# Seven-product weight pairs in a decoder layer: four sums kept in PSUM, weight sums on VectorE

## Chip, core and metric

One core of a Trainium2 chip runs the whole layer as one program. The metric is the device time of one execution in microseconds. The core has five engines that run side by side, each through its own queue in order: TensorE (PE, matmuls into the PSUM banks), VectorE (DVE), ScalarE (ACT), GpSimd (POOL, which has no part in PSUM work here) and SyncE (SP), which here issues almost all DMAs.

## What is computed

A decoder layer for 1024 prompt positions and 8 samples, so 1032 columns, 1024 wide. One input projection (1024 x 6912) feeds three branches (window attention, a state-space layer, a gated MLP); each branch is read out, merged by sigmoid gates and projected, with a layer norm at the end. The part that matters here is the projection:

```
proj = jnp.einsum('ntd,de->nte', x, w_in)
q, k, v, z_a, u_b, z_b, u_c, v_c, z_c, g = jnp.split(proj, cuts, axis=-1)
...
vn = _layernorm(v_c);  y_c = u_c * (tril(W_s) vn + b);   silu(z_c) * y_c
gates = jax.nn.sigmoid(g)
```

## The kernel before

Every product is float32 made of three passes: an operand is split into a high part (an ACT copy to fp32r) and a low part (the difference), and `mm3` (L98) adds high x high, high x low and low x high in one PSUM bank. The high and low parts of a 128x512 weight come from `hilo` (L138): the ACT copy is L145, the subtraction L146 on whichever engine is given. Raw weights are loaded by SP into a pool of 5 buffers (`wraw`, L131), and split weights lie in 4 buffers each ("wh", "wl") or, every second one, in parts of the x tiles that are no longer needed ("strips", L952, L956; the trace names those `b`).

The order of execution is made by a scheduler that simulates the engines and takes instructions by priority, which is the order of the text except where `tc.high_priority()` lifts it. The result is one fixed list for each engine. A wait at the head of a list holds up all behind it.

In time the stages are: projections and the state-space layer (to about us 300); attention, with single projection chunks as filler (`fill`, L760; the attention's own DVE line that scales the scores is L731); then, from us 413 to 702, 13 "pairs"; then the readout and the output projection. Each pair computes two blocks of 128 output columns over all 1032 positions as a 2 x 2 block product (blocks of 512 inputs by 516 positions) in Winograd's form: seven products in place of eight. `half_sums` (L890) and L930 to L937 make the four sums of x beforehand (`Tx`). `pair` (L960) forms four sums of weights: s3 = a11 - a21, s1 = a21 + a22, s2 = s1 - a11, s4 = a12 - s2, all on POOL (trace line L263). A product (`prod`, L976) is two halves of 258 columns, one in a bank of the pool "mm" (3 banks), one in "ms" (4 banks), each with 12 matmuls. Every product takes new banks. The seven additions that make the four output blocks, each in two halves, are `add` (L1007, trace line L1010) on DVE: SBUF plus PSUM to SBUF tiles in `stg` (L948); only the first product P1 is copied out by ACT (L1019). The kinds of pairs are: two "v" (stored as they are), four "zu" (silu of `z` times `u`: ACT L999, DVE L1000 and L1004), seven "g" (tanh on ACT, L990, then stored, L991). `mid` and `ends` place the pieces of the gated MLP (L1055 to L1126) between the pairs.

Of the kernel before, what the change touches and what calls it, by code (L numbers as in the profile page):

```python
# [15 lines left out]
AF = mybir.ActivationFunctionType  # L16
OP = mybir.AluOpType
# [47 lines left out]
def decoder_step(ctx, tc, io):  # L65
    nc = tc.nc
    V, S, G, PE = nc.vector, nc.scalar, nc.gpsimd, nc.tensor
# [7 lines left out]
    pk = ctx.enter_context(tc.tile_pool(name="pk", bufs=4, space=bass.MemoryType.PSUM))  # L75
# [3 lines left out]
    def nm(s):  # L79
        cnt[0] += 1  # L80
        return f"{s}{cnt[0]}"

    def b2(dt=F32):
        return big.tile([128, B2], dt, tag="b2", name=nm("b"))

    def bank(pool=None, n=512):
        if pool is pk:
            t = pk.tile([128, 512], F32, tag="ms", name=nm("ms"), bufs=NMS)
        elif pool == "t":
            t = pk.tile([128, 512], F32, tag="mt", name=nm("mt"), bufs=NMT)  # L90
        else:
            t = pm.tile([128, 512], F32, tag="mm", name=nm("mm"), bufs=NMM)
        return t

    def ct(w=CW, rows=128):
        return tp.tile([rows, CW], F32, tag="ct", name=nm("ct"))

    def mm3(out, pairs, start=True, stop=True):  # L98
        n = len(pairs)
        for i, (ah, al, bh, bl) in enumerate(pairs):  # L100
            PE.matmul(out, ah, bh, start=start and i == 0, stop=False)  # L101
            PE.matmul(out, ah, bl, start=False, stop=False)  # L102
            PE.matmul(out, al, bh, start=False, stop=stop and i == n - 1)  # L103

    def f(ap):
        return ap.bitcast(F32)
# [101 lines left out]
    for k in range(8):  # L208
        for b in range(2):
            hi, lo = fgr[b][k // 4]  # L210
            ws = slice((k % 4) * 128, (k % 4) * 128 + 128)
            for c in range(NCH):
                ps = first[b * 3 + c][:, :CW]
# [48 lines left out]
    def TT(out, a, b, op, eng=None):  # L262
        (eng or V).tensor_tensor(out, a, b, op=op)  # L263
# [168 lines left out]
    for Er_, Ei_, base in ((Eb[:, 1], Eb[:, 0], 1), (Ea[:, 0], Ea[:, 1], 5)):  # L432
        V.memset(Er_[:, :, 0], 1.0)
        V.memset(Ei_[:, :, 0], 0.0)
        for lv in range(4):
            w = 1 << lv
# [5 lines left out]
    for n in (1, 2, 3, 4):  # L442
        o = cv[:, 0, :, n - 1]
# [3 lines left out]
        o = cv[:, 1, :, n - 1]  # L447
# [25 lines left out]
    us_ = [b2(), b2()]  # L473
# [173 lines left out]
    with tc.high_priority():  # L647
        for hf_ in range(2):
            tps = bank("t")
            for i in range(4):  # L650
                m = hf_ * 4 + i
# [91 lines left out]
    def values(m):  # L743

        q0, zo = NS + m * 128, (m % 2) * 1024
        z4 = v2(qzt[:, zo + 512:zo + 1024], 128)
        o = bank(pk)
        k_ = keys(m)[0] // 128
        for kb in range(k_, 2):
            for g in range(2):  # L750
                seq(PE.matmul(o[64 * g:64 * g + 64, :], vtok[:, m - 1 + kb, 64 * g:64 * g + 64],
                              scs[m % 2][:, g * 4:g * 4 + 4, kb * 128:(kb + 1) * 128], start=kb == k_, stop=kb == 1))
        done = V.scalar_tensor_tensor(z4, v2(o, 128), 0.5, z4, op0=OP.mult, op1=OP.mult)
        nc.sync.dma_start(yaD[:, :, q0:q0 + 128], z4)
        return done
# [52 lines left out]
    for i in range(4):  # L808
        for g in range(2):
            rs = slice(64 * g, 64 * g + 64)  # L810
            h = i + 4 * g
# [76 lines left out]
    HT, QT = T // 2, T // 4  # L888
# [9 lines left out]
    for m in range(NBLK):  # L898
# [16 lines left out]
        done = values(m)  # L915
# [15 lines left out]
    for n_, t_ in ((2, tf[2]), (3, tf[0]), (1, tf[1]), (4, tf[3])):  # L931
        h_, l_ = b2(F32R), b2(F32R)
        for k in range(4):
            o = slice(k * HT, (k + 1) * HT)
# [14 lines left out]
    stgs = [[stg[:, (2 * n_ + c) * QT:(2 * n_ + c + 1) * QT] for c in range(2)] for n_ in range(4)]  # L949
# [2 lines left out]
    strips = [tuple(x_[j][:, e * T + HT:e * T + HT + 512] for x_ in (xh, xl)) for j in range(2) for e in range(2)]  # L952
    wcnt = [0]
    mark = []

    def whl(raw, eng):  # L956
        wcnt[0] += 1
        return hilo(raw, eng, strips[wcnt[0] // 2 % 4] if wcnt[0] % 2 else None)

    def pair(kind, n1, n2, mid=()):  # L960
        i11, i12, i21, i22 = 2 * n1, 2 * n1 + 1, 2 * n2, 2 * n2 + 1
        a11, a21 = wraw(i11)[0], wraw(i21)[0]
        s3 = wraw()
        TT(s3, a11, a21, OP.subtract, G)
        a22 = wraw(i22)[0]
        TT(a21, a21, a22, OP.add, G)
        s1 = a21
        s2 = wraw()
        TT(s2, s1, a11, OP.subtract, G)
        w11 = whl(a11, G)  # L970
        a12 = wraw(i12)[0]
        s4 = wraw()
        TT(s4, a12, s2, OP.subtract, G)
        w2 = whl(s2, V)

        def prod(w, n_):  # L976
            ps = [bank()[:, :QT], bank(pk)[:, :QT]]
            for c in range(2):
                mm3(ps[c], [(w[0][:, k * 128:(k + 1) * 128], w[1][:, k * 128:(k + 1) * 128]) + bop(n_, k, c)
                            for k in range(4)])  # L980
            return ps

        p1, u2, c11, u3 = stgs

        done = {}

        def out(m, h, c, t_):
            hs_ = slice(h * HT + c * QT, h * HT + (c + 1) * QT)
            if kind == "g":
                S.activation(t_, t_, AF.Tanh, scale=0.5)  # L990
                nc.sync.dma_start(gD[(n1, n2)[m] - GG][:, hs_], t_)  # L991
                return
            if kind == "v":
                nc.sync.dma_start(vcD[:, (n1, n2)[m] - GVC, hs_], t_)
                return

            if m == 0:
                tg = ct()
                S.activation(tg[:, :QT], t_, AF.Tanh, scale=0.5)  # L999
                V.scalar_tensor_tensor(t_, tg[:, :QT], 1.0, t_, op0=OP.add, op1=OP.mult)  # L1000
            done[m, h, c] = t_
            if (1 - m, h, c) in done:
                z_, u_ = done[0, h, c], done[1, h, c]
                V.scalar_tensor_tensor(u_, z_, 0.5, u_, op0=OP.mult, op1=OP.mult)  # L1004
                nc.sync.dma_start(uszD[:, n1 - GZC, hs_], u_)

        def add(o, a, b):  # L1007
            for c in range(2):
                with tc.high_priority():
                    V.tensor_tensor(o[c], a[c], b[c], op=OP.add)  # L1010

        def outs(m, h, t_):
            for c in range(2):
                out(m, h, c, t_[c])

        ps = prod(w11, (0, 0))
        for c in range(2):
            with tc.high_priority():
                mark.append(S.activation(p1[c], ps[c], AF.Copy))  # L1019
        add(u2, p1, prod(w2, 2))  # L1020
        add(c11, p1, prod(whl(a12, G), (1, 0)))
        outs(0, 0, c11)
        for fn, a_ in mid:
            fn(a_)
        add(u3, u2, prod(whl(s3, V), 3))
        ps = prod(whl(s1, V), 1)
        add(p1, u3, ps)
        outs(1, 1, p1)
        add(u2, u2, ps)
        add(u3, u3, prod(whl(a22, G), 4))  # L1030
        outs(1, 0, u3)
        add(u2, u2, prod(whl(s4, V), (1, 1)))
        outs(0, 1, u2)
        stgs[:] = [c11, u3, u2, p1] if kind == "zu" else [c11, p1, u3, u2]

    prs = [("v", GVC + i, GVC + i + 1) for i in (0, 2)] + [("zu", GZC + i, GUC + i) for i in range(4)]
    prs += [("g", GG + i, GG + i + 1) for i in range(NSTD, 24, 2)]
# [196 lines left out]
    for i in range(4):  # L1234
        gr = gran(GR_GLU + i)
        for c in range(NCH):
            ps = bank()
# [28 lines left out]
    for k4 in range(0, 8, 4):  # L1266
        for n in range(2):
            for k in range(k4, k4 + 4):
                o = slice((k % 2) * 1024 + n * 512, (k % 2) * 1024 + n * 512 + 512)
                PE.matmul(sps[n][32 * (k % 4):32 * (k % 4) + 32, :], msv[:, k], wrs[k // 2][:, o], start=k < 4, stop=k >= 4)  # L1270
    for n in range(2):
        for k in range(8):
            o = slice((k % 2) * 1024 + n * 512, (k % 2) * 1024 + n * 512 + 512)
# [6 lines left out]
    for t in (1, 2, 3, 0, 4, 5, 6, 7, 8):  # L1280
# [7 lines left out]
        for p0, w in ((0, 512), (512, 256), (768, 256)) if last else ((0, 512), (512, 512)):  # L1288
            n, cs = p0 // 512, slice(p0, p0 + w)
            ps = None if t == 0 else bank()[:, 0:w]  # L1290
# [23 lines left out]
        for e0, e1 in ((0, 512), (512, 1024)) if last else ((0, 1024),):  # L1314
            hs_ = slice(e0, e1)
            V.scalar_tensor_tensor(r[:, hs_], r[:, hs_], s6[0:rows, 24:25], lno[0:rows, hs_],
                                   op0=OP.subtract, op1=OP.mult)
            V.scalar_tensor_tensor(r[:, hs_], r[:, hs_], s6[0:rows, 27:28], lno[0:rows, 1024:2048][:, hs_],
                                   op0=OP.mult, op1=OP.add)
# [111 lines left out]
```

## Time and profile before

| | before |
|---|---|
| median of 3 runs | 960.81 us (960.2 to 960.89) |
| the profiled execution | 963.6 us, its span 961.8 us |
| PE busy | 941.6 us (98%) |
| DVE, ACT, POOL busy | 689.5, 366.4, 255.5 us (72, 38, 27%) |
| mean granted TensorE clock | 0.996 |

The span runs from the first to the last instruction. PE's busy time says how much of it has a matmul in flight; the views by stretch tell in which stages it has not, and the waits name what ended such an idle time. An engine that is idle elsewhere costs nothing by itself.

### The profile page before, as it was taken

The page shows a single profiled execution, that of the slowest core. Times are in us where ns is not written, and L with a number is a line of the kernel's source. Part 1 is how long each engine was busy: PE and PEld are TensorE (multiplying, and loading weights), DVE is VectorE, ACT ScalarE, POOL GpSimd, SP SyncE. Part 2 cuts the span into 40 slices and gives each one's busy share as a digit, 9 for nine tenths or more (in the row PEclk, how much of TensorE's full clock was granted, in tenths as well). Part 3 has the DMA queues.
Part 4 walks back from the last instruction along what each step waited for, and adds up shares of the span by engine and source line. Part 5 has one row for each costly group of instructions (what it writes and reads, how often), then busy time and mean ns, then how long its engine had stood idle before and what let it go on. Part 6 is the DMA issues. An engine that isn't in the chain of part 4 may idle for free. (4 is left out here: it accounts for less than half of the span.)

```text
span 961.8 us, 17199 instructions
## 1 busy us (share of the span) xinstructions
PE 941.6 (98%) x6417; PEld 897.9 (93%) x6417; DVE 689.5 (72%) x1476; ACT 366.4 (38%) x839; POOL 255.5 (27%) x225
## 2 busy tenths in 40 slices
PE   8999999999999999999999999999999999999997
PEld 7999999999999888799999999999999999986886
DVE  6687499999986678965567766666657736884754
ACT  5322374444445764842222233333434415350000
POOL 0240000000011112055344544544322782201311
PEclk9999999999999999999999999999999999999999
DMA  8345823525438632244432344554887415421411
GB/s 305 115 138 141 221 77 101 163 87 141 117 115 267 186 89 70 85 122 127 126 91 77 84 140 133 141 150 138 256 273 264 154 55 209 178 73 61 133 66 65
DMA packets 118579, 133.07 MB, mean 138 GB/s; under 512 B 38856, under 2 KB 89416, under 8 KB 117216
## 3 DMA queue, kind: packets, MB, share of 16 engines
q1 hardware_dynamic: 114304, 125.90, 42.9%
q10 hardware_dynamic: 4192, 6.08, 2.0%
q8 instruction: 50, 0.82, 0.4%
q14 instruction: 33, 0.27, 0.1%
HBM read 92.65 MB, written 38.97 MB: 137 GB/s over the span
## 5 line engine op out<-in xcount | busy, mean ns | idle before, releaser
L101 PE MATMUL mm<-b,wh 128*128 128x344 f32 (+1 forms) x996 | 313.7, 315 | 3.4 <-DVE b L1010 1.4
L102 PE MATMUL mm<-b,wh 128*128 128x344 f32 (+1 forms) x996 | 312.1, 313 | 0.0
L103 PE MATMUL mm<-b,wl 128*128 128x344 f32 (+1 forms) x996 | 312.1, 313 | 0.0
L101 PEld LDWEIGHTS mm<-b,wh 128*128 128x128 f32 x996 | 187.5, 188 | 4.5 <-ACT wh L145 1.6
L102 PEld LDWEIGHTS mm<-b,wh 128*128 128x128 f32 x996 | 187.5, 188 | 0.0
L103 PEld LDWEIGHTS mm<-b,wl 128*128 128x128 f32 x996 | 187.4, 188 | 0.0
L146 POOL TENSOR_TENSOR wl<-wr,wh 128x512 fp32r<-128x512 f32 x59 | 85.2, 1445 | 383.2 <-ACT wh L145 377.9
L145 ACT ACTIVATE wh<-wr 128x512 fp32r<-128x512 f32 x129 | 80.7, 626 | 142.1 <-PE mm L102 53.9
L102 PE MATMUL mm<-b,b 128*128 128x258 f32 (+2 forms) x320 | 103.8, 325 | 0.0
L103 PE MATMUL mm<-b,b 128*128 128x258 f32 (+2 forms) x320 | 103.6, 324 | 0.0
L101 PE MATMUL mm<-b,b 128*128 128x258 f32 (+2 forms) x306 | 100.3, 329 | 2.6 <-DVE b L1010 2.6
L146 DVE TENSOR_TENSOR wl<-wr,wh 128x512 fp32r<-128x512 f32 x70 | 56.0, 801 | 50.4 <-ACT wh L145 50.1
L263 POOL TENSOR_TENSOR wr<-wr,wr 128x512 f32<-128x512 f32 x52 | 69.2, 1331 | 80.6 <-DMA wr<-wg 26.5
L102 PEld LDWEIGHTS mm<-b,b 128*128 128x128 f32 x320 | 60.4, 189 | 6.9 <-DVE b L1189 0.8
L101 PEld LDWEIGHTS mm<-b,b 128*128 128x128 f32 x306 | 57.7, 189 | 9.5 <-DVE b L1010 3.4
L103 PEld LDWEIGHTS mm<-b,b 128*128 128x128 f32 x320 | 60.4, 189 | 6.0 <-issue 0.8
L102 PE MATMUL ms<-b,b 128*128 128x258 f32 (+1 forms) x216 | 61.0, 283 | 0.0
L103 PE MATMUL ms<-b,b 128*128 128x258 f32 (+1 forms) x200 | 56.5, 283 | 0.0
L263 DVE TENSOR_TENSOR b<-b,b 128x512 f32<-128x512 f32 (+6 forms) x112 | 53.7, 515 | 1.4 <-ACT b L935 0.4
L263 DVE TENSOR_TENSOR b<-b 128x512 f32<-128x512 f32 (+6 forms) x93 | 52.8, 573 | 0.9
L101 PE MATMUL ms<-b,b 128*128 128x258 f32 (+1 forms) x186 | 52.6, 283 | 0.0
L101 PE MATMUL ms<-b,wh 128*128 128x258 f32 x180 | 51.0, 283 | 0.0
(259 smaller groups left out, 1901.7 us busy)
## 6 DMA issues: line engine op xcount, KB each, us to landing
wr<-wg SPq DMA_DIRECT2D x136, 256.0 KB, 2.9
b<-gD SPq DMA_DIRECT2D x12, 1032.0 KB, 7.6
gD<-b SPq DMA_DIRECT2D x56, 129.0 KB, 3.3
gD<-ct SPq DMA_DIRECT2D x30, 172.0 KB, 1.8
b<-xT SPq DMA_DIRECT2D x4, 1032.0 KB, 9.4
b<-wo SPq DMA_DIRECT2D x4, 1024.0 KB, 5.0
b<-xp SPq DMA_DIRECT2D x8, 512.0 KB, 3.5
b<-xT SPq DMA_DIRECT2D x7, 516.0 KB, 7.7
```

What stands on the lines that cost most here:

```text
L101: PE.matmul(out, ah, bh, start=start and i == 0, stop=False)
L102: PE.matmul(out, ah, bl, start=False, stop=False)
L103: PE.matmul(out, al, bh, start=False, stop=stop and i == n - 1)
L145: S.activation(hi, raw, AF.Copy)
L146: (eng or lo_eng[0]).tensor_tensor(lo, raw, f(hi), op=OP.subtract)
L263: (eng or V).tensor_tensor(out, a, b, op=op)
```

## The change

The seven products come in another order and only three bank pairs, held for all 13 pairs, take them. P1 goes to bank 1 and is copied out by ACT; s2's product is then added by the matmuls onto what bank 1 holds, giving U2 = P1 + P; ACT copies that too; s3's is added onto it (U3) and DVE adds it to P5; at last a22's is added, and the finished block is read from the bank by its consumer (ACT's tanh or copy, or DVE's product with z). Bank 3 takes s1's product (P5, copied by ACT) and then s4's on top, which DVE adds to U2. Bank 2 takes a12's, which DVE adds to P1. The banks change places from pair to pair. The four weight sums and the low parts of a11, a12 and a22 move from POOL to DVE. What the output functions issue is now of high priority.

```diff
-    def mm3(out, pairs, start=True, stop=True):
+    def mm3(out, pairs, start=True, stop=True, **kw):
...
-        TT(s3, a11, a21, OP.subtract, G)
+        TT(s3, a11, a21, OP.subtract, V)
-        TT(a21, a21, a22, OP.add, G)
+        TT(a21, a21, a22, OP.add, V)
-        TT(s2, s1, a11, OP.subtract, G)
-        w11 = whl(a11, G)
+        TT(s2, s1, a11, OP.subtract, V)
+        w11 = whl(a11, V)
-        TT(s4, a12, s2, OP.subtract, G)
+        TT(s4, a12, s2, OP.subtract, V)
...
-        def prod(w, n_):
-            ps = [bank()[:, :QT], bank(pk)[:, :QT]]
+        def prod(w, n_, ps, start=True):
             for c in range(2):
                 mm3(ps[c], [(w[0][:, k * 128:(k + 1) * 128], w[1][:, k * 128:(k + 1) * 128]) + bop(n_, k, c)
-                            for k in range(4)])
-            return ps
-        p1, u2, c11, u3 = stgs
+                            for k in range(4)], start=start, skip_group_check=not start)
+        if not bks:
+            bks.extend([bank()[:, :QT], bank(pk)[:, :QT]] for _ in range(3))
+        bk1, bk2, bk3 = bks
+        bks[:] = [bk2, bk3, bk1]
+        p1, u2, p5, c21 = stgs
...
-        def out(m, h, c, t_):
+        def out(m, h, c, t_, src=None):
+            src = t_ if src is None else src
             if kind == "g":
-                S.activation(t_, t_, AF.Tanh, scale=0.5)
+                S.activation(t_, src, AF.Tanh, scale=0.5)
             if kind == "v":
+                if src is not t_:
+                    S.activation(t_, src, AF.Copy)
...
-                V.scalar_tensor_tensor(u_, z_, 0.5, u_, op0=OP.mult, op1=OP.mult)
+                V.scalar_tensor_tensor(u_, z_, 0.5, us_, op0=OP.mult, op1=OP.mult)
-        def add(o, a, b):
+        def take(o, ps):
+            r_ = []
             for c in range(2):
                 with tc.high_priority():
-                    V.tensor_tensor(o[c], a[c], b[c], op=OP.add)
+                    r_.append(S.activation(o[c], ps[c], AF.Copy))
+            return r_
+        def add(o, ps):
+            for c in range(2):
+                with tc.high_priority():
+                    V.tensor_tensor(o[c], o[c], ps[c], op=OP.add)
-        def outs(m, h, t_):
+        def outs(m, h, t_, src=(None, None)):
+            with tc.high_priority():
...
-        ps = prod(w11, (0, 0))
-        add(u2, p1, prod(w2, 2))
-        add(c11, p1, prod(whl(a12, G), (1, 0)))
-        outs(0, 0, c11)
+        prod(w11, (0, 0), bk1)
+        mark.extend(take(p1, bk1))
+        prod(whl(a12, V), (1, 0), bk2)
+        add(p1, bk2)
+        outs(0, 0, p1)
+        prod(w2, 2, bk1, False)
+        take(u2, bk1)
         for fn, a_ in mid:
             fn(a_)
-        add(u3, u2, prod(whl(s3, V), 3))
-        ps = prod(whl(s1, V), 1)
-        add(p1, u3, ps)
-        outs(1, 1, p1)
-        add(u2, u2, ps)
-        add(u3, u3, prod(whl(a22, G), 4))
-        outs(1, 0, u3)
-        add(u2, u2, prod(whl(s4, V), (1, 1)))
+        prod(whl(s1, V), 1, bk3)
+        take(p5, bk3)
+        prod(whl(s3, V), 3, bk1, False)
+        add(p5, bk1)
+        outs(1, 1, p5)
+        prod(whl(s4, V), (1, 1), bk3, False)
+        add(u2, bk3)
         outs(0, 1, u2)
-        stgs[:] = [c11, u3, u2, p1] if kind == "zu" else [c11, p1, u3, u2]
+        prod(whl(a22, V), 4, bk1, False)
+        outs(1, 0, c21, bk1)
+        if kind == "zu":
+            stgs[:] = [u2, p1, p5, c21]
```

## Rows read from the trace of the kernel before

**Rows 1.** The page's head: the span, and busy time and instructions by engine.

```profile
span 961.8 us, 17199 instructions
PE 941.6 (98%) x6417; PEld 897.9 (93%) x6417; DVE 689.5 (72%) x1476; ACT 366.4 (38%) x839; POOL 255.5 (27%) x225
```

**Rows 2.** Stretches of the pairs: length, busy of PE, PEld, DVE, ACT, POOL, PEclk, DMA.

```profile
413.00:485.00 72.00, 72.00 (x593) 70.31 (x591) 38.20 (x68) 19.76 (x40) 38.65 (x29) 1.00 0.44 133
485.00:572.00 87.00, 82.76 (x675) 81.04 (x673) 63.30 (x118) 25.35 (x55) 38.62 (x32) 1.00 0.32 90
572.00:702.00 130.00, 130.00 (x1078) 130.00 (x1077) 83.67 (x156) 46.15 (x102) 58.34 (x50) 1.00 0.57 167
```

**Rows 3.** Timeline of PE in a g pair: start, length in us, line, operation.

```profile
608.95 0.28 PE L102 MATMUL mm<-b,wh 128*128 128x258 f32 x1
...
611.59 0.28 PE L103 MATMUL ms<-b,wl 128*128 128x258 f32 x1
```

**Rows 4.** PE's waits, us 413 to 702: total us, times, longest.

```profile
PE mm L101 <- DVE b L1010: 4.2, 6, 1.4
```

**Rows 5.** Timeline of PE around one wait; brackets: idle before, releaser.

```profile
531.08 0.28 PE L103 MATMUL ms<-b,b 128*128 128x258 f32 x1
532.72 0.39 PE L101 MATMUL mm<-b,wh 128*128 128x258 f32 x1 [1.36 <-DVE b L1010]
532.94 0.29 PE L102 MATMUL mm<-b,wh 128*128 128x258 f32 x1
```

**Rows 6.** Timelines of SP, POOL, ACT, DVE before that wait.

```profile
524.27 0.33 SPq L134 DMA_DIRECT2D wr<-wg  x1
...
527.18 1.28 POOL L263 TENSOR_TENSOR wr<-wr,wr 128x512 f32<-128x512 f32 x1 [2.94 <-DMA wr<-wg]
...
530.98 0.63 ACT L145 ACTIVATE wh<-wr 128x512 fp32r<-128x512 f32 x1 [6.51 <-POOL wr L263]
...
531.64 0.69 DVE L146 TENSOR_TENSOR wl<-wr,wh 128x512 fp32r<-128x512 f32 x1 [6.31 <-ACT wh L145]
```

**Rows 7.** Timelines of ACT and PE at the two other long waits.

```profile
511.52 0.63 ACT L145 ACTIVATE wh<-wr 128x512 fp32r<-128x512 f32 x1 [4.05 <-DMA wr<-wg]
...
516.25 0.39 PE L101 MATMUL mm<-b,b 128*128 128x258 f32 x1 [0.96 <-DVE b L1010]
...
558.58 0.63 ACT L145 ACTIVATE wh<-wr 128x512 fp32r<-128x512 f32 x1 [6.29 <-DMA wr<-wg]
...
561.58 0.39 PE L101 MATMUL mm<-b,b 128*128 128x258 f32 x1 [1.25 <-DVE b L1010]
```

**Rows 8.** Groups by line: busy us, mean ns; for L146 also min/median/max ns.

```profile
L1010 DVE TENSOR_TENSOR b<-b,ms 128x258 f32<-128x258 f32 x91 | 36.5, 413 | 5.8 <-PE ms L103 5.8
...
L263 POOL TENSOR_TENSOR wr<-wr,wr 128x512 f32<-128x512 f32 x49 | 65.2, 1330 | 80.4 <-DMA wr<-wg 26.5 <-DVE b L1010 8.7 <-DVE b L1000 6.2
...
L146 DVE TENSOR_TENSOR wl<-wr,wh x70: 658/686/1596, 4.2 to 663.8; 128x512 fp32r<-128x512 f32 x70
...
L146 DVE TENSOR_TENSOR b<-wr,b 128x512 fp32r<-128x512 f32 x26 | 26.0, 1002 | 27.3 <-ACT b L145 27.3
```

**Rows 9.** Timeline of ACT in a g pair.

```profile
591.31 0.37 ACT L1019 ACTIVATE b<-mm 128x258 f32<-128x258 f32 x1
596.62 0.63 ACT L145 ACTIVATE b<-wr 128x512 fp32r<-128x512 f32 x1 [4.94 <-POOL wr L263]
597.15 0.37 ACT L1019 ACTIVATE b<-ms 128x258 f32<-128x258 f32 x1
```

**Rows 10.** The attention's end: two stretches (columns as above), timelines of POOL and PE.

```profile
360.00:380.00 20.00, 19.22 (x130) 17.28 (x128) 15.54 (x45) 9.72 (x29) 5.18 (x4) 1.00 0.24 67
400.00:413.00 13.00, 11.14 (x70) 9.24 (x67) 12.93 (x33) 11.72 (x30) 0.34 (x1) 1.00 0.16 49
...
376.48 2.68 POOL L263 TENSOR_TENSOR wr<-wr,wr 128x512 f32<-128x512 f32 x2
...
408.26 1.12 PE L740 MATMUL ms<-ident,b 128*128 128x128 f32 x4 [1.86 <-DVE b L731]
```

More of the change, by code (lines that the diff above doesn't have):

```diff
@@ L96, in ct @@
         return tp.tile([rows, CW], F32, tag="ct", name=nm("ct"))
-    def mm3(out, pairs, start=True, stop=True):
+    def mm3(out, pairs, start=True, stop=True, **kw):
         n = len(pairs)
         for i, (ah, al, bh, bl) in enumerate(pairs):
-            PE.matmul(out, ah, bh, start=start and i == 0, stop=False)
-            PE.matmul(out, ah, bl, start=False, stop=False)
-            PE.matmul(out, al, bh, start=False, stop=stop and i == n - 1)
+            PE.matmul(out, ah, bh, start=start and i == 0, stop=False, **kw)
+            PE.matmul(out, ah, bl, start=False, stop=False, **kw)
+            PE.matmul(out, al, bh, start=False, stop=stop and i == n - 1, **kw)
     def f(ap):
@@ L954, in decoder_step @@
     mark = []
+    bks = []
     def whl(raw, eng):
@@ L1000, in out @@
                 V.scalar_tensor_tensor(t_, tg[:, :QT], 1.0, t_, op0=OP.add, op1=OP.mult)
-            done[m, h, c] = t_
+            done[m, h, c] = t_, src
             if (1 - m, h, c) in done:
-                z_, u_ = done[0, h, c], done[1, h, c]
-                V.scalar_tensor_tensor(u_, z_, 0.5, u_, op0=OP.mult, op1=OP.mult)
+                z_, (u_, us_) = done[0, h, c][0], done[1, h, c]
+                V.scalar_tensor_tensor(u_, z_, 0.5, us_, op0=OP.mult, op1=OP.mult)
                 nc.sync.dma_start(uszD[:, n1 - GZC, hs_], u_)
-        def add(o, a, b):
+        def take(o, ps):
+            r_ = []
@@ L1008, in add @@
             for c in range(2):
                 with tc.high_priority():
-                    V.tensor_tensor(o[c], a[c], b[c], op=OP.add)
-        def outs(m, h, t_):
+                    r_.append(S.activation(o[c], ps[c], AF.Copy))
+            return r_
+        def add(o, ps):
             for c in range(2):
-                out(m, h, c, t_[c])
-        ps = prod(w11, (0, 0))
-        for c in range(2):
+                with tc.high_priority():
+                    V.tensor_tensor(o[c], o[c], ps[c], op=OP.add)
@@ L1018, in pair @@
+        def outs(m, h, t_, src=(None, None)):
             with tc.high_priority():
-                mark.append(S.activation(p1[c], ps[c], AF.Copy))
-        add(u2, p1, prod(w2, 2))
-        add(c11, p1, prod(whl(a12, G), (1, 0)))
-        outs(0, 0, c11)
+                for c in range(2):
+                    out(m, h, c, t_[c], src[c])
+        prod(w11, (0, 0), bk1)
[4 more added lines that the diff above has]
+        prod(w2, 2, bk1, False)
```

## The prediction

> **What bounds the kernel now.** I read the page's head first [rows 1]: TensorE (PE) shows 941.6 of 961.8 us busy, so at most 20 us of the span, about 2%, are not matmul time, and only what lies in that idle time can be won by an edit that leaves the matmuls alone. The change does leave them alone: a pair is seven products of 24 matmuls of 258 columns before and after, 168 in all.
>
> Second, the busy times by stretch over the 13 pairs, us 413 to 702 [rows 2]. In 413 to 485 and in 572 to 702 PE is busy for the whole stretch at a granted clock of 1.00 (2.4 GHz). Only 485 to 572 has holes: 82.76 of 87 us. These are the later of the four pairs that make gates and `u` ("zu" below) and the hand-over to the sigmoid pairs ("g").
>
> Third, the cadence [rows 3]: from 608.95 to 611.59 us 22 matmuls follow each other, so one takes 0.120 us and a product of 24 takes 2.88 us. No stretch runs faster, so the full stretches hold nothing for this change.
>
> Fourth, PE's waits over the pairs [rows 4]: one line, six waits, 4.2 us, all for the VectorE (DVE) additions of L1010. The wait is for a PSUM bank. An example [rows 5]: the matmul at 531.08 is followed by one at 532.72, 1.64 us later where 0.12 is usual, and the next starts 0.22 later. The idle column counts from the modelled end of a matmul, 0.28 us after its start, so a wait costs its idle time, plus 0.28 - 0.12 = 0.16, plus 0.10 at the restart. All six cost 4.2 + 6 x 0.26 = 5.8 us. That is the ceiling for the pairs, 0.6% of the time.
>
> Fifth, why the additions were late [rows 6]: a weight load was issued at 524.27; GpSimd (POOL), after waiting 2.94 us for it, began a weight sum of 1.28 us at 527.18, the first of its three instructions up to 530.9; ScalarE (ACT) made the high part at 530.98 after 6.51 us idle, DVE the low part at 531.64 after 6.31 us idle. The additions that free banks stood behind that low part in DVE's queue. Two other long stalls, at 515 and 560, begin with ACT waiting 4.05 and 6.29 us for a load [rows 7], which held up DVE in the same way; PE idled 0.96 and 1.25 us there.
>
> **The change part by part.** *Additions.* Before, a pair has 14 additions on DVE at 0.413 us [rows 8] and two ACT copies of 0.37 [rows 9]. After, there are six additions and six copies: DVE gives up 8 x 0.413 = 3.30 us a pair, ACT takes 4 x 0.37 = 1.48. The last product of a pair is no longer added; its consumer reads PSUM, which for "g" replaces an SBUF read by a PSUM read and for the first two pairs ("v") adds two ACT copies, 0.74 us. ACT is busy 46.15 of 130 us in the g pairs [rows 2], so this fits.
>
> *Weight sums and low parts.* Four sums leave POOL, where one takes 1.330 us [rows 8], and go to DVE. A sum on DVE of this shape isn't in the trace as such; the nearest row is the low part, the same two-input subtraction of 128x512, 0.686 us at the median with extremes of 0.658 and 1.596. I take 0.686 and keep 0.658 to 1.596 for the bounds. Three low parts of the seven also move, so DVE takes on 7 x 0.686 = 4.80 us a pair (4.6 to 11.2). The sequence behind a load gets shorter by 0.64 us for each sum and about as much for each low part; three of them lie between the load and the end of the low part in rows 6, about 1.9 us.
>
> *DVE in total.* 4.80 - 3.30 = +1.5 us a pair of 21.5. Against it stands that the 26 low parts written over the x tiles average 1.002 us instead of 0.686 [rows 8], and the long ones lie beside POOL work. The Trainium skill, "SBUF — State Buffer", section "Who interferes with whom", says that a GpSimd instruction and a VectorE instruction with two SBUF inputs exclude each other for a whole instruction. By that rule the stretch disappears with POOL's work, and the trace's extremes agree (0.658 alone, 1.596 at most). Going by rows alone, four low parts a pair return between nothing and 4 x 0.32 = 1.3 us, and DVE comes out between +1.5 and +0.2 us a pair. DVE was busy 63.3 of 87 us in the stretch with the holes [rows 2], 73%; +1.5 us in 21.5 makes 80%. It does not become the bound by its sum.
>
> *Waits.* An accumulating product must wait until its bank has been read. In the new order each bank is used again after one other product: P1 is copied by ACT before product 3 adds to its bank, product 3 before 5, product 4 before 6, and product 5 is added by DVE before 7. A half of a product is 12 matmuls or 1.44 us; from the end of a half to the first matmul that reuses its bank is 1.5 products, or 36 x 0.12 = 4.32 us. Before, three "mm" banks in rotation gave 7.2 us and four "ms" banks 10.1. So the room for one late engine falls to 4.3 us, but only one of the four tight readers is on DVE. Behind a waiting copy on ACT stand the high parts and the tanh; behind a waiting sum on DVE the low parts and additions. The sums wait for loads, and what waits for those is now the DVE queue and no longer an engine that was otherwise idle.
>
> *Order.* The second product now takes the plain weight `a12`, and the three-sum weight `s2` comes third, 2.88 us later against its load. The stall at 531 cost 1.52 + 0.10 = 1.6 us; the 1.9 us of sequence or the 2.88 us of order covers it by itself, so I count it gone. Of the other five, 5.8 - 1.6 = 4.2 us, the three short ones (5.8 less the three long ones at about 1.6, 1.5 and 1.2 us leave 1.5) come where DVE is dense, with additions between stretched instructions; eight fewer additions a pair take these away. The two that begin with a late load, 2.7 us, have their cause in a load queue that the change doesn't touch; I count half. Saved: 1.6 + 1.5 + 1.3 = 4.4 us (between 0 and 5.8).
>
> *Before the pairs.* The first pair's three sums run on POOL inside the attention stage (the last two at 376.48 [rows 10]) and go to DVE, which is full at that stage's end, 12.93 of 13 us in 400 to 413, while PE waits 1.86 us for it at 408.26 [rows 10]. 3 x 0.686 = 2.06 us if all of it ends in that wait, 0 if it fits into the 4.5 us that DVE has free in 360 to 380 (15.54 busy of 20). I take 0.7, since the sums are ready in the freer part.
>
> *New waits.* 0 to 9.8 us (rival 2 works out the upper end); I take 0.5.
>
> *Sum:* -4.4 + 0.7 + 0.5 = -3.2 us. The pairs' end starts the readout, whose loads are issued as the pairs' buffers come free, so I pass this on in full. Against the profiled execution: 963.6 - 3.2 = 960.4 us; that execution is 2.8 us slower than the median of the runs, 960.81. The forecast for the median is 960.8 - 3.2 = 957.6 us.
>
> **Rivals.** *1. The stalls stay.* Late loads are the first cause, the load queue is the same, and a bank now has less room. For it: rows 7; against it: the shorter sequence. Then only the stall at 531 is gone, -1.6, against +0.7 and +0.5: 960.4 us, within 0.2% of before.
>
> *2. ACT's copies come late: slower.* Place: the copies of products 1, 3 and 4, queued on ACT behind a high part whose raw weight isn't ready. The ACT rows [rows 9] show it: the copy of one half of P1 runs at 591.31, the high part behind it waits 4.94 us until 596.62, and the copy of the other half, whose matmuls end about 1.44 us after the first's, at 592.75, ends at 597.52, 4.77 us after. With 7.2 us or more of room PE didn't feel it. In the new order it has 4.32, so PE would stand 0.45 us, with sync and restart about 0.75. It decides from a wait on ACT that ends more than 3.9 us after the half. If each of the 13 pairs has one such copy, 13 x 0.75 = 9.8 us are lost, and 960.8 - 4.4 + 0.7 + 9.8 = 966.9 us. Against it: this wait was for POOL's sums, which get faster by 0.64 us each. The Trainium skill, "PSUM — Partial Sum Buffer", section "PSUM bank collisions raise a hardware error", asks that accesses be guarded by whole banks, which speaks against accumulating in a bank that is read between: no half of the copy can overlap the next product. By that rule the 4.32 us is firm; no run before shows a matmul that adds to a bank already read.
>
> *3. It doesn't do what it says.* If the products go out in another order than written, or a full bank is cleared again, the additions go as before and only POOL's work moves; then the time is near rival 1.
>
> **How the numbers follow.** A difference under about 0.2%, 1.9 us, can't be told from none; the limits are 958.9 and 962.7. Forecast with its range 954.8 to 958.9 (all stalls gone, 955.0, at its end): 0.50. Rivals 1 and 3, 958.9 to 962.7: 0.31. Rival 2 in any size above: 0.19. The range must leave out no more than 0.2; I take 954.4 to 964.0, which leaves out the upper part of rival 2 (about 0.12) and a little below. Faster 0.50, same 0.31, slower 0.19.
>
> **What would show it.** PE busy all of the stretch of the four zu pairs, and the wait line on L1010 gone or under 2 us: the saving is right. A new line of PE waiting for ACT's copy, or for the addition of product 5, at cadence breaks spread over the g pairs: rival 2. DVE idle behind a sum that waits for a load: rival 1. In 376 to 413 the wait for L731 grown by more than 1 us: the cost before the pairs is mis-sized. Low parts back at 0.69 us on average would show the stretch gone. A time under 955.0 would mean that the pairs' matmuls themselves go faster than 0.120 us, or that another stage gains, and I have no term for either.

## The result and the profile after

The changed kernel takes 955.27 us (median of 5 runs, 954.23 to 956.12) against 960.81: a ratio of 0.9941 [0.9929, 0.9954], 5.5 us faster. The forecast was 957.6, the range 954.4 to 964.0: sign and range were right, and the gain came out 1.7 times as large. The profiled execution is the one of 955.27 us, span 953.5. First the page's head, as [rows 1]:

```profile
span 953.5 us, 17097 instructions
PE 938.1 (98%) x6417; PEld 895.9 (94%) x6417; DVE 681.9 (72%) x1463; ACT 391.1 (41%) x895; POOL 127.5 (13%) x134
```

POOL lost half its work, ACT took on 25 us, and DVE, to which the sums and low parts went, has 7.6 us less than before. The 6417 matmuls are the same and in the same stages, so a stage can be timed by the start of its first matmul on PE's timeline (numbers 2401, 2662 and 4936 of 6417):

| us | before | after |
|---|---|---|
| attention's end (2401 to 2662) | 44.95 | 44.04 |
| pairs (2662 to 4936) | 280.26 | 275.19 |
| from there to the last matmul | 262.67 | 262.85 |

That is 0.9 + 5.1 - 0.2 = 5.8 us. The rest of the 8.3 us between the two spans lies in the first 25 us of the profiled execution of before (its matmul 101 starts at 24.4 instead of 21.8 us; from us 12 to 16 its granted clock was 0.57 in the mean, in after 1.00). The change doesn't touch that stretch, and the medians don't show the difference.

Second the stretches that answer [rows 2] and [rows 10], columns as there (the last two are the attention's end):

```profile
410.00:482.00 72.00, 71.19 (x583) 69.50 (x582) 41.35 (x76) 26.45 (x57) 0.00 (x0) 1.00 0.45 136
482.00:561.00 79.00, 79.00 (x661) 78.76 (x660) 53.78 (x108) 31.28 (x68) 2.21 (x6) 1.00 0.37 107
561.00:690.00 129.00, 129.00 (x1074) 129.00 (x1073) 79.41 (x134) 56.02 (x124) 9.71 (x16) 1.00 0.54 156
357.00:377.00 20.00, 20.00 (x136) 18.25 (x134) 15.59 (x48) 10.89 (x32) 2.58 (x2) 1.00 0.27 78
397.00:410.00 13.00, 10.48 (x64) 9.34 (x64) 13.00 (x29) 11.09 (x27) 0.00 (x0) 1.00 0.16 49
```

The holes of the zu pairs are gone (79.00 of 79). A small one is new in the first stretch, and PE's waits name it; the wait of [rows 4] has no line any more, and the attention's wait for L731 is as long as before:

```profile
PE ms L740 <- DVE b L731: 2.6, 2, 1.9
...
PE ms L101 <- ACT b L1019: 0.8, 1, 0.8
```

The new wait, on the timelines of SP, ACT and PE (start, length, brackets: idle before and releaser):

```profile
416.40 0.62 SPq L1063 DMA_DIRECT2D b<-sgu  x1
...
418.44 0.33 SPq L134 DMA_DIRECT2D wr<-wg  x1
...
425.07 0.63 ACT L145 ACTIVATE wh<-wr 128x512 fp32r<-128x512 f32 x1 [5.21 <-DMA wr<-wg]
425.61 0.37 ACT L1019 ACTIVATE b<-ms 128x258 f32<-128x258 f32 x1
...
424.93 0.28 PE L103 MATMUL mm<-b,b 128*128 128x258 f32 x1
426.02 0.39 PE L101 MATMUL ms<-b,b 128*128 128x258 f32 x1 [0.81 <-ACT b L1019]
```

A weight load stands on SP behind the constants of the gated MLP (L1063 to L1067). ACT waits 5.21 us for it, the copy of the bank waits behind that high part on ACT, and PE stands 1.09 us from the start of one matmul to the start of the next, where 0.12 is usual. That is rival 2 to the letter, in one place and not in thirteen.

Third the groups that answer [rows 8], over us 408 to 690:

```profile
L263 DVE TENSOR_TENSOR wr<-wr,wr 128x512 f32<-128x512 f32 x49 | 33.7, 687 | 12.4 <-DMA wr<-wg 11.9
L146 DVE TENSOR_TENSOR b<-wr,b 128x512 fp32r<-128x512 f32 x46 | 31.4, 686 | 14.1 <-ACT b L145 12.4 <-PE ms L102 0.8
L145 ACT ACTIVATE wh<-wr 128x512 fp32r<-128x512 f32 x47 | 29.7, 632 | 53.0 <-PE ms L102 38.6 <-DMA wr<-wg 7.0 <-issue 6.1
L1019 ACT ACTIVATE b<-mm 128x258 f32<-128x258 f32 x39 | 15.1, 386 | 34.2 <-PE mm L103 24.6 <-issue 9.6
```

A sum on DVE takes 0.687 us (I took 0.686), the low parts over the x tiles are back from 1.002 to 0.686, a PSUM copy takes 0.37 to 0.39. The third row matters most. Its counterpart in the kernel before, over us 413 to 702:

```profile
L145 ACT ACTIVATE wh<-wr 128x512 fp32r<-128x512 f32 x48 | 29.8, 623 | 68.0 <-POOL wr L263 27.3 <-DMA wr<-wg 22.2 <-PE ms L102 9.7
```

There ACT waited mostly for POOL's sums and for loads. Now it waits mostly for PE (38.6 of 53.0 us), that is for a weight buffer to come free: most weights are ready as early as the buffers allow.

The loads come earlier too. SP issues one when a buffer for raw weights is free, and those are freed by the sums and low parts. What SP's weight loads (L134) waited for longest, before (us 396 to 702) and after (us 396 to 692): total us, times, longest:

```profile
SPq L134 <- POOL wr L263: 60.4, 15, 9.2
```

```profile
SPq L134 <- DVE wr L263: 37.9, 12, 6.7
```

The load at 524.27 in [rows 6], behind which the stall at 531 began, was issued as a low part on POOL ended:

```profile
522.74 1.50 POOL L146 TENSOR_TENSOR b<-wr,b 128x512 fp32r<-128x512 f32 x1
```

### The profile page after: what moved, and what is told of

It is laid out like the page before. It is cut to its first block, busy times and chain, and to the rows that moved or that the text cites. A ratio compares the mean times of both kernels' runs of the same rounds, so it can differ in the third digit from the quotient of the medians.

```text
span 953.5 us, 17097 instructions
## 1 busy us (share of the span) xinstructions
PE 938.1 (98%) x6417; PEld 895.9 (94%) x6417; DVE 681.9 (72%) x1463; ACT 391.1 (41%) x895; POOL 127.5 (13%) x134
## 4 chain that ended last, share of the span: by engine, by line
PE 92%; DVE 4%; DMA 1%; ACT 1%; issue 1%; SPq 0%; DVEq 0%; ACTq 0%
PE mm L101 21%; PE mm L102 20%; PE mm L103 20%; PE ms L101 6%; PE ms L102 6%; PE ms L103 6%; PE mm L775 2%; PE mm L772 2%; PE mm L776 2%; PE ms L751 1%; PE ms L1288 1%; DVE b L894 1%; PE mt L1140 1%; DMA wr<-wg 1%; PE ms L716 1%
## 5 line engine op out<-in xcount | busy, mean ns | idle before, releaser
L146 POOL TENSOR_TENSOR wl<-wr,wh 128x512 fp32r<-128x512 f32 x40 | 56.6, 1416 | 369.9 <-ACT wh L145 360.8
L146 DVE TENSOR_TENSOR wl<-wr,wh 128x512 fp32r<-128x512 f32 x89 | 61.5, 692 | 27.9 <-ACT wh L145 26.8
L102 PEld LDWEIGHTS mm<-b,b 128*128 128x128 f32 x320 | 60.4, 189 | 7.0 <-DVE b L1207 0.8
L263 DVE TENSOR_TENSOR b<-b,b 128x512 f32<-128x512 f32 (+6 forms) x112 | 53.1, 509 | 1.0
L263 DVE TENSOR_TENSOR b<-b 128x512 f32<-128x512 f32 (+6 forms) x93 | 52.8, 574 | 0.9
L101 PE MATMUL ms<-b,wh 128*128 128x258 f32 x180 | 51.0, 284 | 0.0
L102 PE MATMUL ms<-b,wh 128*128 128x258 f32 x180 | 50.8, 282 | 0.0
```

What stands on the lines that cost most here:

```text
L101: PE.matmul(out, ah, bh, start=start and i == 0, stop=False, **kw)
L102: PE.matmul(out, ah, bl, start=False, stop=False, **kw)
L146: (eng or lo_eng[0]).tensor_tensor(lo, raw, f(hi), op=OP.subtract)
```

## The experiments

The four parts of the change are product order with accumulation, sums to DVE, low parts to DVE, and priority; the first three were taken apart. All times are medians; each ratio is against the kernel before on the same chip. Stage times are counted as above and, like the number of PE waits, come from the one profiled execution of each kernel.

| | time, us | ratio, 95% | attention's end | pairs | PE waits in the pairs |
|---|---|---|---|---|---|
| after | 955.27 | 0.9941 [0.9929, 0.9954] | 44.04 | 275.19 | 1 |
| e1_after_pool | 955.35 | 0.9947 [0.9934, 0.9959] | 45.04 | 274.16 | 0 |
| e2_before_dve | 956.00 | 0.9943 [0.9931, 0.9956] | 44.04 | 273.93 | 0 |
| e3_before_order | 957.25 | 0.9963 [0.9949, 0.9976] | 46.48 | 275.30 | 1 |
| f1_before_sums | 954.95 | 0.9942 [0.9929, 0.9956] | 44.02 | 274.34 | 0 |
| f2_before_lows | 954.62 | 0.9939 [0.9924, 0.9953] | 45.03 | 273.84 | 0 |
| e6_late_loads | 955.27 | 0.9940 [0.9927, 0.9952] | 44.03 | 274.18 | 0 |
| f3_tight | 954.86 | 0.9943 [0.9928, 0.9957] | 45.33 | 274.02 | 0 |
| f4_dve_dummy | 963.21 | 1.0025 [1.0014, 1.0036] | 44.01 | 280.90 | 6 |
| f5_after_dummy | 957.40 | 0.9966 [0.9949, 0.9983] | 45.46 | 274.27 | 0 |
| h1_after_act | 955.18 | 0.9944 [0.9927, 0.9961] | 45.49 | 274.16 | 0 |
| h2_dve_act | 955.96 | 0.9949 [0.9936, 0.9963] | 45.59 | 273.93 | 0 |
| g1_late_tx | 950.44 | 0.9891 [0.9876, 0.9907] | 40.19 | 274.19 | 0 |

**The new order and accumulation alone**: the changed kernel with its sums and the three low parts back on GpSimd.

```diff
-        TT(s3, a11, a21, OP.subtract, V)
+        TT(s3, a11, a21, OP.subtract, G)
...
-        w11 = whl(a11, V)
+        w11 = whl(a11, G)
```

> The changed kernel with the four weight sums and the low parts of a11, a12 and a22 back on GpSimd; accumulation in the banks, copies by ScalarE and product order stay. Theory A (late weights: the saving comes from the weight work leaving GpSimd): the stalls for late weights come back, 959 to 962 us, with PE waiting for ScalarE's copies in place of VectorE's additions. Theory B (fewer additions in front of the banks): the stalls stay away, 955 to 956 us.

955.35 us, no PE wait in the pairs. So the stalls go without moving anything off GpSimd. What is lost against the change is in the attention: 45.04 against 44.04 us.

**The move to VectorE alone**: the kernel before with sums and low parts on DVE; 14 additions, order and banks as before.

```diff
-        TT(s3, a11, a21, OP.subtract, G)
+        TT(s3, a11, a21, OP.subtract, V)
...
-        add(u3, u3, prod(whl(a22, G), 4))
+        add(u3, u3, prod(whl(a22, V), 4))
```

> The kernel before with only the weight sums and the three low parts moved to VectorE; fourteen additions a pair in fresh banks and the old order stay. Theory A: about 955 to 957 us, the waits on the additions of L1010 under 1.5 us. Theory B: VectorE gets 4.8 us more a pair and the additions come later still, 961 to 966 us.

956.0 us, again no wait, 273.93 us for the pairs. So the stalls go without any accumulation as well. In the pairs the two halves of the change each buy the whole; they don't add up.

**The product order alone**, additions and GpSimd's work as before:

```diff
-        add(u2, p1, prod(w2, 2))
         add(c11, p1, prod(whl(a12, G), (1, 0)))
         outs(0, 0, c11)
+        add(u2, p1, prod(w2, 2))
...
-        add(u3, u3, prod(whl(a22, G), 4))
-        outs(1, 0, u3)
         add(u2, u2, prod(whl(s4, V), (1, 1)))
         outs(0, 1, u2)
+        add(u3, u3, prod(whl(a22, G), 4))
+        outs(1, 0, u3)
...
```

> The kernel before with the new order of the products alone (P1, a12, s2, s1, s3, s4, a22); additions on VectorE and weight work on GpSimd stay. If the order hid the stall at 531, 1.6 us of 5.8 are gone: 959 us. Theory A and B in their pure form: 960 to 961.5 us, no change.

957.25 us, below every figure expected. PE's waits over its pairs:

```profile
PE mm L101 <- DVE b L1010: 0.9, 1, 0.9
```

Five of six waits are gone, the stall at 531 with them; one is left, at 557.16, 1.16 us from start to start. (Of its 46.48 us at the attention's end some 1.5 are not the order's; see the last section.)

**Half of the move each**: only the four sums, or only the three low parts, to DVE.

```diff
...
-        TT(s2, s1, a11, OP.subtract, G)
+        TT(s2, s1, a11, OP.subtract, V)
...
```

> The kernel before with only the four weight sums of a pair on VectorE; the low parts of a11, a12, a22 stay on GpSimd, order and additions as before. If the three sums in sequence behind a load are the cause (3 x 0.64 = 1.9 us sooner): all stalls gone, 955 to 956 us, and the first pair's sums no longer stretch the score scaling of L731 at 375 (0.9 us). If the low parts matter as much: 957.5 to 959 us.

```diff
-        w11 = whl(a11, G)
+        w11 = whl(a11, V)
...
```

> The kernel before with only the low parts of a11, a12, a22 on VectorE; the sums stay on GpSimd, order and additions as before. If the sums' sequence is the cause: 959.5 to 961 us, stalls at 531 and 560 stay, and L731 keeps its 4.29 us at 375. If GpSimd's queue as a whole is the cause (three instructions fewer in it): 956 to 957 us.

954.95 and 954.62 us, no wait in either; the second lies below both of its expected ranges, so the three low parts alone are enough. One thing tells the two apart, the attention's end: 44.02 with the sums on DVE, 45.03 with the sums still on POOL.

**The new wait**: the changed kernel with the MLP's constants loaded in pieces after pairs 1, 2 and 3.

```diff
-    behind(nc.sync.dma_start(lnp[:, 0:1536], io["sgu"]), mark[1])
...
+            behind(nc.sync.dma_start(lnp[:, o:o + 512], io["sgu"][:, o:o + 512]), mark[2 * n_ + 1])
```

> The changed kernel with the gated MLP's constants (768, 256 and 64 KB) loaded in pieces after pairs 1, 2 and 3 and no longer all at once after P1 of pair 0. If the one new wait in the pairs (PE for ScalarE's copy at 424.93, 1.1 us, behind a weight load that took 6.6 us among those loads) is theirs: 954.1 us, and that wait is gone. If another load takes their place: 955.3 us, as the changed kernel.

With those loads moved the wait is gone and the pairs take 274.18 in place of 275.19 us. The median, 955.27 again, doesn't show that 1 us; the runs of one kernel spread over 2 us.

**Less room for a bank**: the changed kernel with s2's product written right behind P1, so that its bank would have to be read within half a product.

```diff
         mark.extend(take(p1, bk1))
+        prod(w2, 2, bk1, False)
+        take(u2, bk1)
         prod(whl(a12, V), (1, 0), bk2)
...
-        prod(w2, 2, bk1, False)
-        take(u2, bk1)
```

> The changed kernel with s2's product directly behind P1, on the same bank, and a12's third: from the end of a half of P1 to the first matmul that adds to its bank 1.44 us in place of 4.32, and s2 needed 2.88 us sooner. Rival 2 (a late copy stops PE): a copy takes 0.37 us and starts about 0.2 us after the half, so a copy in time costs nothing; where ScalarE is held by a high part (0.63 us or more) PE waits: 13 pairs x 0.3 to 1.0 us, 959 to 968 us. If ScalarE is always free for the copy: 955 to 956 us.

954.86 us and no wait, but the case of 1.44 us did not arise: on PE's timeline the scheduler had put a half of a12's product between the two. For one half of P1 the room shrank to one product, some 2.9 us; for the other it stayed at 4.3.

**GpSimd disturbing VectorE**: for each of the 91 split weights a useless GpSimd addition of 128x512, once beside the unaccumulated kernel with everything on DVE (f4) and once beside the changed one (f5).

```diff
-        return hilo(raw, eng, strips[wcnt[0] // 2 % 4] if wcnt[0] % 2 else None)
+        hl = hilo(raw, eng, strips[wcnt[0] // 2 % 4] if wcnt[0] % 2 else None)
+        G.tensor_tensor(scr, f(hl[0]), f(hl[0]), op=OP.add)
+        return hl
...
```

> The kernel before with sums and low parts on VectorE (which took 956.0 us) and, for each split weight, one GpSimd addition of 128x512 that reads the high part and whose result nobody uses: nothing waits for GpSimd, but it is as busy as before, 7 x 1.33 us a pair. If exclusion between GpSimd and VectorE (stretched low parts, 1.00 in place of 0.69 us) made the stalls: low parts stretched again and 959 to 962 us. If the sequence of sums made them: low parts stretched, but 955.5 to 957 us.

> The changed kernel with a useless GpSimd addition of 128x512 that reads each split weight's high part (91 of them). The same additions put beside the kernel before with its sums and low parts on VectorE gave 963.2 us, six PE waits of 5.5 us on VectorE's additions and 280.9 us for the pairs. Theory A (what counts is how much VectorE does between a weight's landing and the additions; the change has eight additions fewer a pair and only one bank whose release needs VectorE before the next but one product): VectorE's busy time is stretched by some 20 us as there, but waits in the pairs stay under 2 us and the time is 955 to 957 us. Theory B (the smaller room of 4.32 us counts more than the fewer additions): at least as many waits as there, now also on ScalarE's copies, 962 to 968 us.

DVE's two groups of weight work, by line, first without the additions (e2), then with them (f4), then the changed kernel with them (f5):

```profile
L263 DVE TENSOR_TENSOR wr<-wr,wr 128x512 f32<-128x512 f32 x52 | 35.8, 689 | 17.6 <-DMA wr<-wg 17.2
L146 DVE TENSOR_TENSOR b<-wr,b 128x512 fp32r<-128x512 f32 x46 | 31.5, 687 | 8.6 <-ACT b L145 8.4
```

```profile
L263 DVE TENSOR_TENSOR wr<-wr,wr 128x512 f32<-128x512 f32 x52 | 45.2, 869 | 15.9 <-DMA wr<-wg 15.7
L146 DVE TENSOR_TENSOR b<-wr,b 128x512 fp32r<-128x512 f32 x46 | 38.4, 836 | 5.5 <-ACT b L145 5.4
```

```profile
L263 DVE TENSOR_TENSOR wr<-wr,wr 128x512 f32<-128x512 f32 x52 | 42.2, 811 | 13.8 <-DMA wr<-wg 13.1
L146 DVE TENSOR_TENSOR b<-wr,b 128x512 fp32r<-128x512 f32 x46 | 37.0, 808 | 18.6 <-ACT b L145 18.2
```

GpSimd's additions stretch DVE's by 18 to 26% in both. In f4 six PE waits come back, the pairs take 7 us more than in e2, and the time, 963.21 us, lies above the range expected from the stretch. PE's waits in f4's pairs:

```profile
PE mm L101 <- DVE b L1014: 5.5, 6, 1.6
```

How, on the timelines of SP, ACT and DVE in f4:

```profile
459.69 0.42 SPq L1134 DMA_DIRECT2D b<-yaD  x1
...
460.74 0.38 SPq L134 DMA_DIRECT2D wr<-wg  x1
...
468.97 0.63 ACT L145 ACTIVATE wh<-wr 128x512 fp32r<-128x512 f32 x1 [9.01 <-DMA wr<-wg]
...
469.63 0.69 DVE L146 TENSOR_TENSOR wl<-wr,wh 128x512 fp32r<-128x512 f32 x1 [8.49 <-ACT wh L145]
470.24 0.42 DVE L1014 TENSOR_TENSOR b<-b,mm 128x258 f32<-128x258 f32 x1
...
471.82 1.54 DVE L146 TENSOR_TENSOR b<-wr,b 128x512 fp32r<-128x512 f32 x1
473.29 1.26 DVE L1004 SCALAR_TENSOR_TENSOR b<-ct,b 128x258 f32<-128x258 f32 x1
474.47 0.41 DVE L1014 TENSOR_TENSOR b<-b,mm 128x258 f32<-128x258 f32 x1
```

The longest stall (PE at 468.84, 1.87 us from start to start) is the mechanism of [rows 6] and [rows 7] again: a late load behind a large one, the high part, the low part, and behind it the addition that frees the bank. The next one (at 473.58, 1.35 us) would not be there without the stretch: 1.54 and 1.26 us where 0.69 and 0.42 are the undisturbed lengths, 1.69 us too many ahead of the addition at 474.47. But the low part at 471.82 comes soon after the late load, so it isn't shown that the stretch makes a stall by itself. The two other long ones (at 438.71 and 480.71, 1.37 and 1.38 us) stand behind sums of the usual 0.69 us that had waited 2.22 and 1.97 us for a load. And e2 has the same large load and its weights came in time: with new instructions the scheduler's lists differ, and 7 us is not the price of the stretch alone.

The changed kernel under the same load (f5) shows no PE wait in its profiled execution, and pairs of 274.27 us. Its runs go from 954.92 to 962.23 us, half of them above 958, and none of that half was profiled. The granted clock of these six is lower, 0.995 in the median against 0.998, which by itself is at most some 3 us (an estimate: 0.003 of 957) of the 4.6 us between the medians of the two halves; that the rest are stalls is likely and not shown. The profile fits theory A, the median lies just above that theory's range and 5.8 us under f4's, on another chip. The changed kernel seems the more robust; which of its parts makes it so, the runs don't separate, and without the disturbance it isn't needed.

**ScalarE disturbed**: two useless copies of 128x512 on ACT behind each high part, beside the changed kernel (h1) and beside e2 (h2).

```diff
+        for _ in range(2):
+            S.activation(scr, f(hl[0]), AF.Copy)
...
```

> The changed kernel with two useless ScalarE copies of 128x512 (0.63 us each) behind each high part of a split weight: ScalarE gets some 115 us more work over the pairs (112 to about 227 of 274). Theory A (rival 2 of the prediction: a bank must now be read within 4.32 us, and four of the readers of a pair are ScalarE's): a copy that finds 1.9 us of high part and useless copies ahead of it, or the wait for a load in front of these, comes too late; PE waits on ScalarE's copies L1019 at several places, 3 to 15 us over the pairs, 958 to 970 us. Theory B (the room is wide enough for ScalarE also with this work, the one wait at 425 is an accident of one load): no more than two waits on ScalarE, 955 to 957 us.

> The kernel before with its sums and low parts on VectorE, and the same two useless ScalarE copies behind each high part. Here only P1 is copied by ScalarE and a bank has 7.2 us of room or more. Theory A (room decides): ScalarE's delay reaches PE only through late high parts, so fewer and shorter PE waits than in the changed kernel with the same useless copies, and none on L1019; 955 to 958 us and at least 2 us below that kernel. Theory B (what decides is how early the weights are ready, which both kernels share): about the same waits in both, now on VectorE's additions, times within 1.5 us of each other.

h1's three stretches of pairs, columns as above, and ACT's groups of high parts over us 408 to 690:

```profile
410.00:482.00 72.00, 72.00 (x581) 70.40 (x580) 42.08 (x76) 60.31 (x118) 0.00 (x0) 0.99 0.45 136
482.00:561.00 79.00, 79.00 (x661) 78.76 (x660) 55.15 (x112) 61.62 (x122) 2.22 (x6) 1.00 0.35 101
561.00:690.00 129.00, 129.00 (x1080) 129.00 (x1079) 79.30 (x134) 93.63 (x195) 9.77 (x16) 1.00 0.52 153
```

```profile
L145 ACT ACTIVATE wh<-wr 128x512 fp32r<-128x512 f32 x47 | 29.6, 629 | 23.6 <-PE ms L102 22.4 <-DMA wr<-wg 1.1
L145 ACT ACTIVATE b<-wr 128x512 fp32r<-128x512 f32 x46 | 28.9, 628 | 19.4 <-PE ms L102 19.0 <-PE mm L776 0.3
```

ACT has almost twice its work, and PE is full in all three stretches: 955.18 us, and 955.96 for h2. Theory B held in both. Even so ACT's high parts still wait for PE's free buffers (22.4 and 19.0 us) and hardly for loads (1.1). The room of 4.32 us was not strained: the copies of the last twelve pairs still end 0.6 to 1.5 us after the half that they read. The one late copy seen in the changed kernel came behind a late load.

**The wait in the attention**: e6 with the high parts of three of the four x sums, and what follows them on DVE, placed behind the last scaling of the scores (`scaled[0]` is the last instruction issued by L731 so far).

```diff
-            S.activation(h_[:, o], t_[:, o], AF.Copy)
+            i1 = S.activation(h_[:, o], t_[:, o], AF.Copy)
+            if n_ in (1, 3, 4):
+                behind(i1, scaled[0])
...
```

> The changed kernel with two delays: the gated MLP's constants are loaded in pieces after pairs 1, 2 and 3 (as in the earlier run, 955.27 us), and the high parts of three of the four x sums, with what follows them on VectorE, are placed behind the last scaling of the scores (L731). The wait of PE for L731 at 402.59 (2.2 us as a gap in the changed kernel, 2.2 us at 406.09 in the kernel before) has VectorE's x sums ahead of it. If these are what makes L731 late: the gap shrinks below 1 us and the time is 953.5 to 954.5 us. If L731 is late by its own chain (scores, ScalarE's exponentials, the sums of a row), the gap stays at about 2 us, the time at 955.3; later x sums could also delay the first pair, which would show as a wait at the pairs' first products, 956 us or more.

950.44 us (949.5 to 951.0): 10.8 us below the kernel before on the same chip, 4.8 below the changed kernel's median on another, and the fastest version here. It lies 3 us under the range expected. DVE's timeline in e6, where PE stops 1.27 us at 396.36 and 2.23 us at 402.64, both for L731:

```profile
395.26 0.69 DVE L263 TENSOR_TENSOR b<-b,b 128x516 fp32r<-128x516 f32 x1
...
396.03 1.28 DVE L263 TENSOR_TENSOR b<-b,b 128x516 fp32r<-128x516 f32 x2
397.22 1.14 DVE L731 TENSOR_SCALAR b<-b,stat 128x256 f32<-128x256 f32 x4
...
399.47 1.91 DVE L263 TENSOR_TENSOR b<-b,b 128x516 fp32r<-128x516 f32 x3
...
404.46 1.14 DVE L731 TENSOR_SCALAR b<-b,stat 128x256 f32<-128x256 f32 x4
```

and in g1, where the same line is L732:

```profile
395.56 1.14 DVE L732 TENSOR_SCALAR b<-b,stat 128x256 f32<-128x256 f32 x4
...
399.62 1.13 DVE L732 TENSOR_SCALAR b<-b,stat 128x256 f32<-128x256 f32 x4
...
401.28 4.93 DVE L263 TENSOR_TENSOR b<-b,b 128x516 fp32r<-128x516 f32 x8
```

Its stretch at the attention's end, columns as above:

```profile
397.00:410.00 13.00, 13.00 (x87) 11.38 (x87) 13.00 (x26) 12.35 (x28) 0.00 (x0) 1.00 0.18 58
```

The scalings run 1.66 and 4.84 us earlier, the low parts of the x sums (L263, 128x516) after them, and PE is busy 13.00 of 13 us. Both stops are gone: 44.03 to 40.19 us, and the pairs don't start late for it (274.19). I had expected only the second stop to go.

## Why the prediction was right, and where it was off

*The bound and the ceiling*: right. The matmuls keep 0.120 us, the floor of the pairs is 273.8 to 274.3 us in ten kernels of different kinds, and what was won was PE's idle time. I had put that at 5.8 us in the pairs; 280.26 - 274.0 = 6.3 is there.

*The stalls, -4.4 expected*: mis-sized; -6.1 came (5.1 net of the 1.0 of the new wait). The step that failed is "I count half" for the two stalls that begin with a late load, whose queue I took to be untouched by the change. It isn't: SP waits for the sums and low parts before it can load, 60.4 us for POOL's sums alone before, 37.9 us for DVE's after, and ACT's waits for loads before these high parts fell from 22.2 to 7.0 us. Nor did I ask how long a stall is against all that precedes it. A stall of 1.2 to 1.6 us stands at the end of a whole sequence: load, POOL's or DVE's work, high part, low part, additions. By the prices of rows 8 (an estimate) e1, e2, f1 and f2 each take a different piece of one to three us off it, and all four are left without a wait; e3, the product order alone, is left with one of six. That the sequence was too long by little fits all five. A rival stays: that the scheduler's list for the kernel before was an unlucky one, and any edit gets another. No run changes the lists alone, so how much is the shorter sequence and how much the new list, the runs don't separate. That each step adds its own share, as my sum had it ("eight fewer additions a pair take these away"), is refuted by f1 and f2, which have all 14 additions and none of those stalls. What a late load can still do, f4's 9.01 us show.

*DVE's total, +0.2 to +1.5 us a pair expected*: wrong sign; -7.6 us over the whole kernel [rows 1 and the head above]. I gave back the stretch only for low parts, four a pair; rows 8 show 26 of them at 1.002 us, which is two a pair, but those in the other buffers were stretched as well (x70: 801 ns in the mean, now 692). What the sum lacked is that the stretch also sat on the lines of `u` and `z`, L1000 (836 ns before, 424 after at L1008) and L1004 (789, now 421), on one of the gated MLP (L1062: 1185, now 790) and on L731. The Trainium skill, "SBUF — State Buffer", section "Who interferes with whom", states that a VectorE instruction with two SBUF inputs contends with a GpSimd instruction that reads SBUF. By that rule DVE's sums should be longer in f4 than in e2, and they are: 869 against 689 ns.

*The attention's end, +0.7 expected*: wrong sign; -0.9 came. Those sums cost DVE nothing net there, because on POOL they had stretched a VectorE line beside them. The scaling that ran beside POOL's sums [rows 10] in before, and the same four in after:

```profile
375.02 4.29 DVE L731 TENSOR_SCALAR b<-b,stat 128x256 f32<-128x256 f32 x4
```

```profile
374.10 1.13 DVE L731 TENSOR_SCALAR b<-b,stat 128x256 f32<-128x256 f32 x4
```

3.16 us longer than by itself, with PE waiting twice behind it (1.05 and 0.95 us from start to start at 378.31 and 380.42; neither is there after, but a stop of 1.30 us at 396.30 is new). In the runs whose TensorE clock held, the stage is 44.0 us wherever the sums are on DVE (after, e2, e6, f1, f4) and 45.0 where they are on POOL (before, e1, f2). I used the rule for the low parts and forgot it for the term two paragraphs below.

*New waits, +0.5 expected*: 1.0 in the profile, by rival 2's mechanism in one place, gone in e6. Rival 2 as a whole fell, and not only because the waits for POOL's sums [rows 9] had gone: e1 keeps those sums and h1 almost doubles ACT's work, and neither has a PE wait in the pairs. Its price was misread besides. The half whose copy starts at 597.15 in [rows 9] was not complete at 592.75 but 2.5 us sooner (counted back from the pairs' last product; PE had not finished a later "mm" half when the first copy began at 591.31). Its last matmul in the kernel before:

```profile
590.06 0.28 PE L103 MATMUL ms<-b,b 128*128 128x258 f32 x1
```

So that copy ended 7.3 us after its half, not 4.77, and by the sum's own rule a bank with 4.32 us of room would have cost PE some 3 us a pair in place of 0.75. That this didn't happen is luck as far as the forecast goes: such late copies did not carry over. In the last twelve pairs of the changed kernel every copy ends 0.6 to 1.3 us after its half, and in e3, with additions, banks and POOL's work as before, the copies of the six last P1 end after at most 2.8 us where before it was up to 7.6.

*Rival 1* (stalls stay) and *rival 3* (not as written) did not occur. Sum by the profile: -6.1 - 0.9 + 1.0, with +0.2 after the pairs, makes -5.8, and it is -5.5 by the medians, in place of -3.2.

*Not in the sum at all*: the 2.2 us stop for L731. I showed it as a place where the change could cost and not as the next thing to win. With the stop before it, it was worth 3.8 us, two thirds of what the whole change brought.

What stays open: whether a new list alone would have done it. The priority for what the output functions issue wasn't tried alone (e2, f1 and f2 reach the floor without it). The room below which an accumulating bank stalls wasn't reached. The slower runs of f5 weren't seen in a profile.

## What to carry to other kernels

When an engine at its cadence floor shows a few short stalls, compare the length of the stalls with the length of the sequence that is late, and ask what frees the buffer that a late load goes into. Here, by the estimate above, each of several edits took more off that sequence than the longest stall, the others bought nothing more, and the simplest would have done for the pairs (f2, three low parts given to another engine). Moving two-input work from GpSimd to VectorE must be costed with what comes back on every VectorE line beside it. And read the waits of the neighbouring stages before rewriting the main one: a few lines of ordering in the attention were worth nearly as much as the rewrite.

## What the runs showed of the hardware

A VectorE instruction with one tensor input was stretched too: the TENSOR_SCALAR of L731 (128x256, with one scalar a partition, four of them) took 4.29 us beside GpSimd's two-input instructions and 1.13 without. Three of the four took 1.38 to 1.42 us each there, and 0.34 without.

Adding matmuls to a bank that has been read in between cost nothing that can be seen: 24 matmuls of a product keep 0.120 us each, and the pairs with accumulation (274.2) and without it (273.9) agree.

After the stop of 2.2 us at L731 the granted clock fell in some executions and not in others. In h1, columns as above, around its stop at 404.65:

```profile
406.00:407.00 1.00, 0.12 (x1) 0.12 (x1) 1.00 (x3) 1.00 (x3) 0.00 (x0) 1.00 0.48 176
407.00:408.00 1.00, 1.00 (x5) 0.62 (x6) 1.00 (x4) 1.00 (x3) 0.00 (x0) 0.75 0.00 0
408.00:409.00 1.00, 1.00 (x6) 1.00 (x5) 1.00 (x3) 0.67 (x2) 0.00 (x0) 0.50 0.00 0
```

The clock is 0.50 (1.2 GHz) for the microseconds after PE has started again, at a cost of about 1.5 us (45.49 against 44.04). Five of the thirteen profiled kernels with that stop show it (e3, f3, f5, h1, h2), the other eight don't, with a stop of the same length. In g1 the stop is gone and the clock stays at 1.00. A stop of PE can thus cost more than its length; why the clock fell after it in some executions only, the runs don't show.
